# A fourth staging place for split weight halves, from the first output projection on, in a two-layer fp32 backbone on one core

## The chip, the cores and the metric

The kernel runs on one core of a Trainium2 chip. The metric is device time in microseconds (us) of one execution; lower is better. Engines are named as in the profile: PE (TensorE matmul), PEld (its weight loads), DVE (VectorE), ACT (ScalarE), POOL (GpSimd) and SP (SyncE, which issues most DMAs).

## What is computed

Two layers with shared weights are applied to two groups of 128 tokens each (256 columns in all), 2048 channels wide:

```
x = x + g1 * mixer(norm(x) * (1 + sc1) + sh1)      # layer 0: HGRN2 recurrence and gMLP, then w_out
                                                    # layer 1: 2-D DFT ("Fourier"), then w_out
up = h @ w_up                                       # 2048 -> 2*5632
conv = pad[:-2]*cw[0] + pad[1:-1]*cw[1] + pad[2:]*cw[2] + cb
gate, val = split(conv);  x = x + g2 * ((silu(gate) * val) @ w_down)
mod = silu(cond) @ mod_w + mod_b                    # sh, sc, g of each layer: 2048 -> 12288
```

A final RMSNorm ends it. Everything is fp32.

## The kernel before

**Weights as a stream.** All weights pass once from HBM through SBUF. A *unit* is a 128x2048 fp32 tile (1 MB, two *halves* of 128x1024), loaded by SP into one of four `raw` places, five from `open_late` on. For accuracy each half is split in two before the matmuls: ACT copies it rounded to fp32r into `wh` (L169), DVE subtracts to get the rest, `wl` (L170). One half then feeds 24 matmuls of 128x256 (L810, function `t_products`): for each of 4 column blocks and 2 row blocks, `wh` with the high part of the activations, `wh` with the low part, `wl` with the high part. `wh` and `wl` have HL_BUFS = 3 places each, so that the copy into a place waits until PE has finished the half that was there.

**Order of the work.** `Stream.run` (L118) walks over the list of steps and emits instructions. Ahead of a half's matmuls it emits the splits of the halves after it (L200: `while state["split"] < min(len(todo), done + HL_BUFS)`). The framework's scheduler then orders each engine's queue; each engine runs its queue in that order. `loads` (L129) puts the next unit into a `raw` place as soon as all that reads the place has been emitted; SP's queue is in order too.

**Other users of the stream.** The modulation weights are units as well. Some go to PE (L455, "mod units"), 60 of the late ones go to DVE: two *pieces* per unit (L470, a multiply-and-sum over 128x2048), which hold the `raw` place until the second piece is done. One piece is emitted per half, ordered behind the latest split (`next_slow`).

**Stages from the change on** (us from the span's start, read from the trace): first output projection from about 495, FFN of layer 0 from 590 to 1402 (three rounds of up groups and a down projection, the down rounds at about 787 to 910, 1094 to 1186 and 1336 to 1402), Fourier stage 1402 to 1455, second output projection to 1550, FFN of layer 1 to 2330, final norm.

**In an FFN up group** the convolution reads a padded tile `z` (three of them, rotated) into a tile `c` (C_BUFS = 4 of them): one ACT and two DVE instructions (L1384, L1388). ACT's silu, two POOL products (L1450, L1453, tile `gate`) and a split into `G` (L716 on ACT, L717 on DVE) follow. In a projection, ACT scales the sums (L1326) and DVE adds them to X (L1328).

**Scratch in the `late` pool** (opened by `open_late` when the mixers' memory is given back): `cw`, `pos` (the position matrices of the Fourier stage), `z`, `raw4`, four `sq4` tiles (squares for the norm), `uy`/`gate`, four `c`, `junk`, two `a3` and two `odd` (Fourier stage).

Of the kernel before, what the change touches and what calls it, by code (L numbers as in the profile page):

```python
# [18 lines left out]
P = 128  # L19
D = 2048  # L20
KD = D // P
T = 256
# [57 lines left out]
class Stream:  # L80
# [2 lines left out]


    def __init__(self, tc, raw_pool, hl_pool):
        self.tc, self.nc, self.hl_pool = tc, tc.nc, hl_pool
        self.last_split = None
        self.pools = {"early": None, "quarter": None}
        self.bufs = {"early": EARLY_BUFS, "quarter": 1}

        self.slots = deque(dict(pool=raw_pool, tag=f"raw{i}", unit=None) for i in range(RAW_BUFS))
        self.steps = []
        self.units = []
        self.place = self.first = 0
        self.bg = deque()
        self.tails = deque()
        self.soon = deque()
        self.slow = deque()
        self.flags = set()
# [23 lines left out]
    def run(self):  # L123
# [37 lines left out]
        def split_next():  # L161
            s = todo[state["split"]]
            raw = s["u"]["tile"]
            if raw is None:
                return False
            wh = self.hl_pool.tile([P, 2, 512], F32R, tag="wh", name="wh")
            wl = self.hl_pool.tile([P, 2, 512], F32R, tag="wl", name="wl")
            r = raw[:, s["half"] * 1024 : (s["half"] + 1) * 1024].rearrange("p (k n) -> p k n", k=2)
            nc.scalar.copy(out=wh, in_=r)  # L169
            self.last_split = nc.vector.tensor_tensor(out=wl, in0=r, in1=wh.bitcast(F32), op=ALU.subtract).ins  # L170
            s["w"] = (wh, wl)
            state["split"] += 1
            used(s)
            return True
# [8 lines left out]
        for s in self.steps:  # L183
# [5 lines left out]
            elif s["kind"] == "raw":  # L189
                loaded(s)  # L190
                s["fn"](s["u"]["tile"])
                used(s)
            elif s["kind"] == "pieces":
                loaded(s)
                pieces, end = s["fn"](s["u"]["tile"])
                self.slow.extend(pieces[:-1])
                self.slow.append(lambda f=pieces[-1], s=s: (f(), used(s)))
                if end:
                    self.slow.append(end)
            else:  # L200
                while state["split"] < min(len(todo), done + HL_BUFS) and split_next():
                    pass
                while "w" not in s:
                    if not split_next():
                        self.next_slow() if self.slow else self.soon.popleft()()
                if s["pre"]:
                    s["pre"]()
                s["fn"](*s.pop("w"))
                done += 1
                for _ in range(1 + (len(self.soon) > 3)):  # L210
                    if self.soon:
                        self.soon.popleft()()
                if self.slow:
                    self.next_slow()
                self.some()
# [43 lines left out]
def backbone_kernel(ctx: ExitStack, tc: tile.TileContext, a: dict):  # L259
# [1 line left out]

    const = ctx.enter_context(tc.tile_pool(name="const", bufs=1))
    raw_pool = ctx.enter_context(tc.tile_pool(name="raw", bufs=1))
    hl_pool = ctx.enter_context(tc.tile_pool(name="hl", bufs=HL_BUFS))
    tmp = ctx.enter_context(tc.tile_pool(name="tmp", bufs=2))
    acc_pool = ctx.enter_context(tc.tile_pool(name="acc", bufs=ACC_BUFS, space=PSUM))
    misc_pool = ctx.enter_context(tc.tile_pool(name="misc", bufs=MISC_BUFS, space=PSUM))
# [329 lines left out]
    def add_square(t):  # L597
# [1 line left out]
        if t == 0:  # L599
            stat["late"] = []  # L600
        if t >= 12:
            sq = late["pool"].tile([P, T], F32, tag="sq4", name="sq4", bufs=4)
            nc.scalar.activation(out=sq, in_=X[:, t], func=AF.Square)
            stat["late"].append(sq)
            return
# [752 lines left out]
    def open_late():  # L1358

        late["pool"] = ctx.enter_context(tc.tile_pool(name="late", bufs=2))  # L1360
        st.slots.append(dict(pool=late["pool"], tag="raw4", unit=None))
        late["cw"] = late["pool"].tile([P, 2 * 88 * 4], F32, name="cw", bufs=1)
        nc.sync.dma_start(out=late["cw"], in_=a["cw"])
        late["pos"] = late["pool"].tile([P, 3, P], F32, name="pos", bufs=1)
        nc.sync.dma_start(out=late["pos"], in_=a["pos"])
        cond_rows()
        late["zs"] = deque()
        for i in range(3):
            z = late["pool"].tile([P, 2, 260], F32, name=f"z{i}", bufs=1)
            nc.gpsimd.memset(z, 0.0)  # L1370
            late["zs"].append(z)

    def put_ffn(layer):
        cw0 = layer * 88 * 4
# [3 lines left out]

        def conv(z, ft):

            c = late["pool"].tile([P, 260], F32, tag="c", name="c", bufs=C_BUFS)
            w = cw0 + 4 * ft
            o = c[:, 0:258]
            nc.scalar.activation(  # L1384
# [97 lines left out]
    def put_fourier():  # L1482
# [4 lines left out]
        def dft(raw):  # L1487
            d.append(late["pool"].tile([P, 2, 4, 256], F32R, tag="wide", name="dft", bufs=1))
            split_pair(d[0], raw[:, 0:1024].rearrange("p (k n) -> p k n", k=4))

        st.call(st.finish_slow)
        st.unit(a["dft"], [dict(kind="raw", fn=dft)])

        def stage1(n):
# [12 lines left out]
                        skip_group_check=True,  # L1507
                    )
            ab = late["pool"].tile([P, 516], F32, tag="gate", name="ab")
            a3 = late["pool"].tile([P, P], F32, tag="a3", name="a3")  # L1510
            nc.scalar.copy(out=ab[:, 0:128], in_=ps[:, 0:128])
            nc.gpsimd.memset(ab[:, 128:129], 0.0)
            nc.scalar.copy(out=ab[:, 129:512], in_=ps[:, 129:512])
# [4 lines left out]
        def stage2(n, ab, a3):  # L1518
# [16 lines left out]
                        stop=(j == len(parts) - 1),  # L1535
                    )
            s = slice(g * P, (g + 1) * P)
            odd = late["pool"].tile([P, 2, P], F32, tag="odd", name="odd")
            nc.scalar.copy(out=odd[:, 1], in_=y[:, 3 * P : 4 * P])
            nc.vector.tensor_tensor(out=odd[:, 0], in0=y[:, 2 * P : 3 * P], in1=odd[:, 1], op=ALU.add)  # L1540
            nc.vector.tensor_tensor(out=odd[:, 1], in0=y[:, 2 * P : 3 * P], in1=odd[:, 1], op=ALU.subtract)
# [26 lines left out]
        for n in range(9):  # L1568
            st.call(lambda n=n: step(n))
            for _ in range(FNET_MODS[n]):  # L1570
                put_mod("raw")
        st.call(cond_rows)

    def finish():
# [183 lines left out]
```

## Time and profile before

| | |
|---|---|
| three runs | 2347.5, 2352.22, 2356.18 us (median 2352.22) |
| the profiled execution | 2348.72 us, its span 2346.9 us |
| PE busy | 2284.4 us (97%) |
| PE weight loads busy | 2126.6 us (91%) |
| DVE busy | 1684.5 us (72%) |
| ACT busy | 1245.1 us (53%) |
| POOL busy | 393.8 us (17%) |
| DMA | 590 MB, 251 GB/s over the span |

Busy is the time in which an engine has at least one instruction running. Matmuls overlap in PE's pipeline, so its idle time alone does not tell how many matmuls a wait has cost. Between rows of a timeline the start times show the pace.

### The profile page before, as it was taken

How to read it: one execution, taken by the hardware profiler on the slowest of the kernel's cores; microseconds unless marked ns; L12 is line 12 of the kernel's file. 1: busy time of each engine (PE TensorE's matmuls, PEld its weight loads, DVE VectorE, ACT ScalarE, POOL GpSimd, SP SyncE). 2: the span in 40 equal slices, each digit the busy share in tenths (PEclk: the TensorE clock that was granted, in tenths of full speed). 3: DMA queues.
4: the chain of work that ended last, by engine and by line, in shares of the span. 5: the costliest groups of instructions: out<-in, count | busy, mean ns of one | idle time of the engine just before them, and what ended most of it. 6: DMA issues, size and time to landing. Idle time of an engine off the chain costs nothing.

```text
span 2346.9 us, 44307 instructions
## 1 busy us (share of the span) xinstructions
PE 2284.4 (97%) x18316; PEld 2126.6 (91%) x18316; DVE 1684.5 (72%) x2370; ACT 1245.1 (53%) x2052; POOL 393.8 (17%) x427
## 2 busy tenths in 40 slices
PE   6999999999999999999999999999999999999997
PEld 4788878788999999999999986999999999999997
DVE  4558977756878887888888777778884556545664
ACT  5337755554755544555455545566554555545554
POOL 0002321322211101110001151222120011100123
PEclk9999999999999999999999999999999999999998
DMA  8977778788567787777877778755665555555552
GB/s 344 390 299 273 262 288 311 265 347 298 197 236 268 258 310 276 270 268 269 307 283 274 268 260 344 280 204 202 235 246 197 180 181 180 183 187 187 181 180 73
DMA packets 88123, 590.09 MB, mean 251 GB/s; under 512 B 9840, under 2 KB 12272, under 8 KB 20336
## 3 DMA queue, kind: packets, MB, share of 16 engines
q1 hardware_dynamic: 84896, 582.01, 66.6%
q10 hardware_dynamic: 3024, 5.24, 0.6%
q8 instruction: 143, 2.34, 0.4%
q14 instruction: 60, 0.49, 0.1%
HBM read 584.07 MB, written 3.15 MB: 250 GB/s over the span
## 4 chain that ended last, share of the span: by engine, by line
PE 80%; DVE 8%; DMA 3%; POOL 3%; ACT 3%; issue 2%; SPq 0%; DVEq 0%; POOLq 0%; ACTq 0%
PE acc L810 69%; PE acc L841 3%; PE modacc L455 3%; DVE wl L170 3%; DVE junk L470 2%; ACT wh L169 1%; PE modacc L403 1%; POOL gate L1450 1%; DMA raw<-in_down 1%; DVE junk L492 1%; PE acc L826 1%; DMA rows<-in_crow 1%; DMA raw<-in_w_out 1%; DVE c L1388 0%; DVE HS L717 0%
## 5 line engine op out<-in xcount | busy, mean ns | idle before, releaser
L810 PE MATMUL acc<-HS,wh 128*128 128x256 f32 x6656 | 1217.6, 285 | 10.5 <-DVE ush L1402 4.9
L170 DVE TENSOR_TENSOR wl<-raw,wh 128x1024 fp32r<-128x1024 f32 x704 | 872.6, 1246 | 409.3 <-ACT wh L169 406.2
L169 ACT CAST wh<-raw 128x1024 fp32r<-128x1024 f32 x704 | 733.7, 1047 | 711.7 <-PE acc L810 549.0
L810 PEld LDWEIGHTS acc<-HS,wh 128*128 128x128 f32 x6656 | 1031.5, 190 | 55.4 <-issue 37.3
L810 PE MATMUL acc<-HS,wl 128*128 128x256 f32 x3328 | 941.4, 283 | 4.0 <-DVE wl L170 3.9
L810 PE MATMUL acc<-G,wh 128*128 128x256 f32 x3840 | 695.8, 284 | 0.1
L810 PEld LDWEIGHTS acc<-HS,wl 128*128 128x128 f32 x3328 | 635.1, 191 | 7.4 <-DVE wl L170 7.1
L810 PEld LDWEIGHTS acc<-G,wh 128*128 128x128 f32 x3840 | 597.5, 192 | 23.7 <-issue 15.9
L810 PE MATMUL acc<-G,wl 128*128 128x256 f32 x1920 | 544.0, 284 | 7.6 <-DVE wl L170 7.4
L810 PEld LDWEIGHTS acc<-G,wl 128*128 128x128 f32 x1920 | 367.5, 192 | 13.7 <-DVE wl L170 13.7
L1450 POOL TENSOR_TENSOR gate<-gate,c 128x128 f32<-128x128 f32 x88 | 98.2, 1116 | 1232.2 <-DVE c L1388 1160.4
L470 DVE SCALAR_TENSOR_TENSOR junk<-raw,rows 128x2048 bf16<-128x2048 f32 x120 | 276.7, 2306 | 0.0
L1388 DVE SCALAR_TENSOR_TENSOR c<-z,cw,c 128x258 f32<-128x258 f32 x352 | 171.3, 520 | 18.2 <-ACT c L1384 15.8
L716 ACT CAST G<-gate 128x256 fp32r<-128x256 f32 x88 | 35.8, 407 | 140.5 <-POOL gate L1453 138.4
L455 PE MATMUL modacc<-raw,cs 128*32 128x512 f32 x704 | 102.8, 613 | 0.4 <-DMA raw<-in_mod 0.4
L1384 ACT ACTIVATE c<-z,cw 128x258 f32<-128x258 f32 x176 | 102.5, 614 | 0.0
L1326 ACT ACTIVATE acc<-acc,mods 128x128 f32<-128x128 f32 x240 | 81.3, 342 | 36.3 <-PE acc L810 30.9
L841 PE MATMUL acc<-wh,HS 128*128 128x512 f32 x256 | 85.7, 404 | 0.0
L492 DVE SCALAR_TENSOR_TENSOR junk<-quarter,rows 128x512 bf16<-128x512 f32 x96 | 73.8, 768 | 14.2 <-DMA quarter<-in_modq 7.8
L717 DVE TENSOR_TENSOR G<-gate,G 128x256 fp32r<-128x256 f32 x88 | 44.9, 511 | 52.6 <-ACT G L716 52.6
L607 POOL TENSOR_TENSOR sq<-X 128x256 f32<-128x256 f32 x48 | 50.1, 1062 | 186.8 <-DVE X L1328 186.8
L723 POOL TENSOR_TENSOR h<-X,rstd 128x256 f32<-128x256 f32 x44 | 41.2, 945 | 239.3 <-DVE HS L717 208.8
(197 smaller groups left out, 1458.0 us busy)
## 6 DMA issues: line engine op xcount, KB each, us to landing
raw<-in_up SPq DMA_DIRECT2D x176, 1024.0 KB, 4.9
raw<-in_mod SPq DMA_DIRECT2D x150, 1024.0 KB, 5.8
raw<-in_down SPq DMA_DIRECT2D x88, 1024.0 KB, 4.8
raw<-in_w_in SPq DMA_DIRECT2D x49, 1024.0 KB, 6.8
raw<-in_w_out SPq DMA_DIRECT2D x32, 1024.0 KB, 7.0
early<-in_mod SPq DMA_DIRECT2D x30, 1024.0 KB, 10.0
quarter<-in_modq SPq DMA_DIRECT2D x24, 512.0 KB, 3.9
raw<-in_w_in SPq DMA_DIRECT2D x14, 512.0 KB, 10.9
```

The lines of the kernel that those rows point to most:

```text
L169: nc.scalar.copy(out=wh, in_=r)
L170: self.last_split = nc.vector.tensor_tensor(out=wl, in0=r, in1=wh.bitcast(F32), op=ALU.subtract).ins
L455: nc.tensor.matmul(ps[0][32 * j : 32 * j + 32, :], lhsT=cs[:, 4 * u + j, 3 - cg : 35 - cg], rhs=raw[:, 512 * j : 512 * j + 512], start=fir ...
L470: nc.vector.scalar_tensor_tensor(out=junk, in0=raw, scalar=1.0, in1=late["rows"][:, g], op0=ALU.mult, op1=ALU.mult, accum_out=mods[:, s, g ...
L492: nc.vector.scalar_tensor_tensor(out=junk, in0=raw[:, 512 * i : 512 * i + 512], scalar=1.0, in1=mx["rows"][:, g], op0=ALU.mult, op1=ALU.mu ...
L607: nc.gpsimd.tensor_tensor(out=sq, in0=X[:, t], in1=X[:, t], op=ALU.mult)
L810: nc.tensor.matmul(ps[b][:, jj * T : (jj + 1) * T], lhsT=w[:, i, c], rhs=rhs(kt)[:, xs], start=(kt == first and n == 0 and jj == 0), stop= ...
L841: nc.tensor.matmul(ps[g][:, :], lhsT=rhs(kt)[:, xs], rhs=w[:, i, :], start=(kt == first and n == 0), stop=(kt == last and n == 2),)
L1326: nc.scalar.activation(out=ps[b][:, s], in_=ps[b][:, s], func=AF.Identity, scale=by)
L1384: nc.scalar.activation(out=o, in_=z[:, 1:259], func=AF.Identity, scale=tap(w + 1), bias=tap(w + 3))
L1388: nc.vector.scalar_tensor_tensor(out=o, in0=z[:, i : i + 258], scalar=tap(w + i), in1=o, op0=ALU.mult, op1=ALU.add)
L1450: nc.gpsimd.tensor_tensor(out=y[:, 0:P], in0=sg[:, 0:P], in1=cv[j + 2][:, 0:P], op=ALU.mult)
```

## The change

From `open_late` on there is a fourth place for `wh` and `wl`. The places become a rotating list of (pool, number), to which `open_late` adds one in the `late` pool, at the front; the splits ahead of a half are emitted up to the list's length. The 8 KB per partition are found by putting `sq4`, `a3` and `odd` into the four `c` tiles, and `pos` into the `z` tile that stands first in the rotation: it is loaded by a DMA on ACT's queue ahead of the Fourier stage (SP loaded it in `open_late` before), and POOL clears that tile behind the stage.

```diff
+        self.split_in = deque((hl_pool, i) for i in range(HL_BUFS))
...
-            wh = self.hl_pool.tile([P, 2, 512], F32R, tag="wh", name="wh")
-            wl = self.hl_pool.tile([P, 2, 512], F32R, tag="wl", name="wl")
+            pool, i = self.split_in[0]
+            self.split_in.rotate(-1)
+            wh = pool.tile([P, 2, 512], F32R, tag=f"wh{i}", name="wh", bufs=1)
+            wl = pool.tile([P, 2, 512], F32R, tag=f"wl{i}", name="wl", bufs=1)
...
-                while state["split"] < min(len(todo), done + HL_BUFS) and split_next():
+                while state["split"] < min(len(todo), done + len(self.split_in)) and split_next():
...
-            sq = late["pool"].tile([P, T], F32, tag="sq4", name="sq4", bufs=4)
+            sq = small()[:, 0:T]
...
+        st.split_in.appendleft((late["pool"], HL_BUFS))
...
-        late["pos"] = late["pool"].tile([P, 3, P], F32, name="pos", bufs=1)
-        nc.sync.dma_start(out=late["pos"], in_=a["pos"])
...
+    def small():
+        return late["pool"].tile([P, 260], F32, tag="c", name="c", bufs=C_BUFS)
...
+        def positions():
+
+            z = late["zs"][0].rearrange("p k n -> p (k n)")
+            late["pos"] = z[:, 0 : 3 * P].rearrange("p (w n) -> p w n", w=3)
+            nc.scalar.dma_start(out=late["pos"], in_=a["pos"])
+
+        st.call(positions)
...
-            a3 = late["pool"].tile([P, P], F32, tag="a3", name="a3")
+            a3 = small()[:, 0:P]
...
-            odd = late["pool"].tile([P, 2, P], F32, tag="odd", name="odd")
+            odd = small()[:, 0:T].rearrange("p (i n) -> p i n", i=2)
...
+        st.call(lambda: nc.gpsimd.memset(late["zs"][0], 0.0))
```

Lines shift by a few: L169, L170, L470, L716, L1326, L1328 of before are L173, L174, L474, L720, L1330, L1332 of the changed kernel. The numbers in the rows below count buffers as they are made; two splits with the same `raw` number are the halves of one unit.

DVE's queue in the first down round (at about 821 us of the trace of before) holds, before:

```order
L170 TENSOR_TENSOR wl_8791<-raw_8682,wh_8790 128x1024
L170 TENSOR_TENSOR wl_8819<-raw_8682,wh_8818 128x1024
L170 TENSOR_TENSOR wl_8849<-raw_8782,wh_8848 128x1024
L470 SCALAR_TENSOR_TENSOR junk_8876,mods_79<-raw_8648,rows_5000 128x2048
L170 TENSOR_TENSOR wl_8879<-raw_8782,wh_8878 128x1024
L470 SCALAR_TENSOR_TENSOR junk_8908,mods_79<-raw_8648,rows_5000 128x2048
L170 TENSOR_TENSOR wl_8913<-raw_8788,wh_8912 128x1024
L470 SCALAR_TENSOR_TENSOR junk_8940,mods_79<-raw_8754,rows_5000 128x2048
```

and in the changed kernel, where raw_8784 and raw_8790 are the units that were raw_8782 and raw_8788:

```order
L174 TENSOR_TENSOR wl_8793<-raw_8656,wh_8792 128x1024
L174 TENSOR_TENSOR wl_8823<-raw_8784,wh_8822 128x1024
L174 TENSOR_TENSOR wl_8851<-raw_8784,wh_8850 128x1024
L474 SCALAR_TENSOR_TENSOR junk_8880,mods_79<-raw_8650,rows_4998 128x2048
L174 TENSOR_TENSOR wl_8883<-raw_8790,wh_8882 128x1024
L474 SCALAR_TENSOR_TENSOR junk_8910,mods_79<-raw_8650,rows_4998 128x2048
L174 TENSOR_TENSOR wl_8915<-raw_8790,wh_8914 128x1024
L474 SCALAR_TENSOR_TENSOR junk_8944,mods_79<-raw_8719,rows_4998 128x2048
```

The pattern of splits and pieces is the same, but each split is that of the next half: both halves of one unit now stand ahead of the first piece, which stood between them.

ACT's queue at the end of the last up group of that round (at about 799 us) holds, before:

```order
L169 CAST wh_8546<-raw_8395 128x1024
L1449 ACTIVATE gate_8610<-c_8542 128x258
L169 CAST wh_8580<-raw_8435 128x1024
L716 CAST G0_2329<-gate_8610 128x256
L169 CAST wh_8616<-raw_8435 128x1024
L169 CAST wh_8650<-raw_8505 128x1024
```

and in the changed kernel (raw_8437 and raw_8507 were raw_8435 and raw_8505):

```order
L173 CAST wh_8550<-raw_8437 128x1024
L1456 ACTIVATE gate_8614<-c_8546 128x258
L173 CAST wh_8582<-raw_8437 128x1024
L720 CAST G0_2329<-gate_8614 128x256
L173 CAST wh_8620<-raw_8507 128x1024
L173 CAST wh_8652<-raw_8507 128x1024
```

Here too the places in the queue are the same and each copy is that of the next half: ahead of the L716 that waits for POOL, both halves of the unit are copied where one was.

ACT's queue at the start of the second output projection (at about 1454 us) holds, before:

```order
L169 CAST wh_15889<-raw_15807 128x1024
L169 CAST wh_15893<-raw_15807 128x1024
L169 CAST wh_15899<-raw_15850 128x1024
L169 CAST wh_15939<-raw_15850 128x1024
L169 CAST wh_15969<-raw_15878 128x1024
L169 CAST wh_15997<-raw_15878 128x1024
L535 ACT_TABLE_LOAD
```

and in the changed kernel:

```order
L173 CAST wh_15889<-raw_15806 128x1024
L173 CAST wh_15893<-raw_15806 128x1024
L173 CAST wh_15899<-raw_15849 128x1024
L173 CAST wh_15903<-raw_15849 128x1024
L173 CAST wh_15945<-raw_15877 128x1024
L173 CAST wh_15973<-raw_15877 128x1024
L539 ACT_TABLE_LOAD
```

Six copies stand ahead of the table load in both, but the fourth (wh_15903 for wh_15939) now belongs to the group that is emitted ahead of the first matmuls and has a free place.

## Rows read from the trace of the kernel before

**Rows 1.** The page: busy us of each engine, its share of the span, instructions.
```profile
PE 2284.4 (97%) x18316; PEld 2126.6 (91%) x18316; DVE 1684.5 (72%) x2370; ACT 1245.1 (53%) x2052; POOL 393.8 (17%) x427
```
**Rows 2.** Waits of PE from 495 us to the end: tile and line that waited <- what ended the wait: us in total, times, longest.
```profile
PE acc L810 <- DVE wl L170: 8.3, 19, 1.3
PE acc L810 <- DVE ush L1402: 4.9, 2, 3.5
PE acc L1501 <- ACT HS L716: 3.0, 3, 1.2
```
**Rows 3.** Timeline of PE at 1352 us: start, us from the first start to the last end, instruction, count, [idle before <- what ended it].
```profile
1352.32 0.40 PE L810 MATMUL acc<-G,wh 128*128 128x256 f32 x2
1353.22 0.39 PE L810 MATMUL acc<-G,wl 128*128 128x256 f32 x1 [0.50 <-DVE wl L170]
1353.44 0.40 PE L810 MATMUL acc<-G,wh 128*128 128x256 f32 x2
1353.68 0.28 PE L810 MATMUL acc<-G,wl 128*128 128x256 f32 x1
```
**Rows 4.** The first wait of Rows 2 in stretches of 100 us, in this order: from 500, 800, 900, 1100, 1300, 1400 and 1700 us.
```profile
PE acc L810 <- DVE wl L170: 0.3, 1, 0.3
PE acc L810 <- DVE wl L170: 0.9, 4, 0.2
PE acc L810 <- DVE wl L170: 0.6, 3, 0.2
PE acc L810 <- DVE wl L170: 1.3, 2, 0.7
PE acc L810 <- DVE wl L170: 3.0, 4, 1.3
PE acc L810 <- DVE wl L170: 1.8, 3, 0.8
PE acc L810 <- DVE wl L170: 0.6, 2, 0.3
```
**Rows 5.** Waits of ACT from 495 us to the end.
```profile
ACT wh L169 <- PE acc L810: 495.3, 300, 4.9
ACT G L716 <- POOL gate L1453: 138.4, 86, 4.7
ACT wh L169 <- DMA raw<-in_down: 50.5, 17, 5.7
ACT wh L169 <- DMA raw<-in_w_out: 9.8, 3, 4.5
```
**Rows 6.** Timelines of ACT, DVE and PE at the end of the last up group of the first round.
```profile
805.25 0.41 ACT L716 CAST G<-gate 128x256 fp32r<-128x256 f32 x1 [4.62 <-POOL gate L1453]
805.56 3.13 ACT L169 CAST wh<-raw 128x1024 fp32r<-128x1024 f32 x3
806.64 1.23 DVE L170 TENSOR_TENSOR wl<-raw,wh 128x1024 fp32r<-128x1024 f32 x1 [0.53 <-ACT wh L169]
811.27 0.39 PE L810 MATMUL acc<-G,wl 128*128 128x256 f32 x1 [0.21 <-DVE wl L170]
```
**Rows 7.** Timelines of ACT and DVE in the first down round.
```profile
827.77 2.00 ACT L169 CAST wh<-raw 128x1024 fp32r<-128x1024 f32 x2 [5.69 <-DMA raw<-in_down]
828.85 1.22 DVE L170 TENSOR_TENSOR wl<-raw,wh 128x1024 fp32r<-128x1024 f32 x1 [5.36 <-ACT wh L169]
830.00 2.28 DVE L470 SCALAR_TENSOR_TENSOR junk<-raw,rows 128x2048 bf16<-128x2048 f32 x1
832.21 1.22 DVE L170 TENSOR_TENSOR wl<-raw,wh 128x1024 fp32r<-128x1024 f32 x1
```
**Rows 8.** Timeline of DVE in the third down round.
```profile
1348.00 1.23 DVE L170 TENSOR_TENSOR wl<-raw,wh 128x1024 fp32r<-128x1024 f32 x1 [3.37 <-ACT wh L169]
1353.08 2.70 DVE L470 SCALAR_TENSOR_TENSOR junk<-raw,rows 128x2048 bf16<-128x2048 f32 x1
1355.71 1.62 DVE L170 TENSOR_TENSOR wl<-raw,wh 128x1024 fp32r<-128x1024 f32 x1
1357.26 2.81 DVE L470 SCALAR_TENSOR_TENSOR junk<-raw,rows 128x2048 bf16<-128x2048 f32 x1
1360.01 1.75 DVE L170 TENSOR_TENSOR wl<-raw,wh 128x1024 fp32r<-128x1024 f32 x1
```
**Rows 9.** Timelines of ACT and PE at the start of the second output projection.
```profile
1453.90 3.10 ACT L169 CAST wh<-raw 128x1024 fp32r<-128x1024 f32 x3
1456.52 0.39 PE L810 MATMUL acc<-G,wl 128*128 128x256 f32 x1 [0.78 <-DVE wl L170]
1469.90 3.62 ACT L535 ACTIVATE rows<-rows 128x4096 f32<-128x4096 f32 x1 [2.70 <-DMA rows<-in_crow]
```
**Rows 10.** Stretches: busy us of PE, PEld, DVE, ACT and POOL with instruction counts, PEclk, DMA share, GB/s; and from the page's costliest groups the mod units' matmuls (busy, mean ns).
```profile
1750.00:2330.00 580.00, 579.42 (x4816) 579.14 (x4815) 334.37 (x377) 305.94 (x504) 67.23 (x84) 1.00 0.50 177
L455 PE MATMUL modacc<-raw,cs 128*32 128x512 f32 x704 | 102.8, 613 | 0.4 <-DMA raw<-in_mod 0.4
```
**Rows 11.** Timelines of DVE and ACT near the end of the last but one up group of layer 0, and the clearing of the three `z` tiles by POOL (busy, mean ns).
```profile
1309.49 0.47 DVE L1388 SCALAR_TENSOR_TENSOR c<-z,cw,c 128x258 f32<-128x258 f32 x1
1311.05 0.41 ACT L716 CAST G<-gate 128x256 fp32r<-128x256 f32 x1 [2.47 <-POOL gate L1453]
L1370 POOL MEMSET z<- 128x520 f32 x3 | 1.5, 532 | 0.1
```

More of the change, by code (lines that the diff above doesn't have):

```diff
@@ L85, in __init__ @@
     def __init__(self, tc, raw_pool, hl_pool):
-        self.tc, self.nc, self.hl_pool = tc, tc.nc, hl_pool
+        self.tc, self.nc = tc, tc.nc
+        self.split_in = deque((hl_pool, i) for i in range(HL_BUFS))
         self.last_split = None
@@ L263, in backbone_kernel @@
     raw_pool = ctx.enter_context(tc.tile_pool(name="raw", bufs=1))
-    hl_pool = ctx.enter_context(tc.tile_pool(name="hl", bufs=HL_BUFS))
+    hl_pool = ctx.enter_context(tc.tile_pool(name="hl", bufs=1))
     tmp = ctx.enter_context(tc.tile_pool(name="tmp", bufs=2))
@@ L1379, in conv @@
         def conv(z, ft):
-            c = late["pool"].tile([P, 260], F32, tag="c", name="c", bufs=C_BUFS)
+            c = small()
             w = cw0 + 4 * ft
```

## The prediction, made before the changed kernel was run

> **What bounds the kernel now.** The page comes first: PE is busy 97% of the span [rows 1]. Its own waits come next, since only they can give anything back. From 495 us on, where the fourth place exists, PE waits 19 times for `wl`, 8.3 us in all, and the other waits are for work that the change leaves in its order: the evacuation of the first up group (4.9 us) and the Fourier stage's activations (3.0 us) [rows 2]. So the kernel is bound by PE, and what a deeper staging can win lies in those 19 waits.
>
> Idle time is not the whole of a wait. In the timeline two matmuls take 0.24 us from start to start, 0.12 each, though one lasts 0.28; the `wl` matmul at 1353.22 follows `wh` matmuls that began at 1352.32, so it came 0.90 - 0.24 = 0.66 us late, of which 0.50 is shown as idle, and the next start is 0.22 behind it instead of 0.12 [rows 3]. Each wait thus costs its idle time plus 0.16 + 0.10 = 0.26 us. Rows 4 list the waits by stretch; with 0.26 each they cost, from 500 us: 0.56; from 800: 1.94; from 900: 1.38; from 1100: 1.82; from 1300: 4.04; from 1400: 2.58; from 1700: 1.12. That is 13.4 us, the most that the fourth place can take away directly [rows 4].
>
> A half takes PE 24 x 0.12 = 2.88 us [rows 3]. That is also what a further place can add to the lead of the splits. The longest single wait, 1.3 + 0.26 us, is shorter [rows 2], but several follow each other, so what delays the splits has to be looked at stretch by stretch. Behind 1750 us PE starts 4816 matmuls in 580 us, again 0.12 us each, without a gap worth naming [rows 10]: that quarter of the kernel cannot move.
>
> **What the change does to the splits.** ACT copies a half when PE has left its place; 300 of its waits (495.3 us) are that one [rows 5]. With three places the copy for the third half waits for the half before the running one; with four, the copy for the fourth half waits for the same moment. The orders of the queues show it: the pattern stays, the split is that of the next half. So splits come 2.88 us earlier for PE wherever the place was what they waited for. Where the weights themselves are late, nothing comes earlier: 20 waits of ACT, 60.3 us, are for the DMA of projection weights [rows 5]. That gives three kinds of stretches.
>
> *Behind a blocked ACT.* In an up group ACT's queue stands up to 4.7 us at L716, waiting for POOL's product, 86 times [rows 5]; the splits behind it are late. At 805.25 such a wait ends, three copies follow, and PE waits at 811.27 [rows 6]. The raw data are there, so one half more in store covers it. Of the waits from 800 us one is of this kind (0.21 + 0.26 = 0.47 us), and I count those from 900 (1.38) and from 1700 (1.12) to it, as both stand in up groups: 2.97 us, all gained. In the second output projection ACT waits 2.70 us for a DMA and then computes 3.62 us at L535 [rows 9]; the two waits of PE that follow are covered too: 2.58 less the first one, 0.78 + 0.26 = 1.04, leaves 1.54 us. That first one stays: it stands where the splits begin after the Fourier stage, at 1453.90, and PE has nothing to run on before [rows 9].
>
> *Weights late, then DVE full.* In the down rounds two DVE pieces per unit (2.28 us each) hold the raw places. At 827.77 ACT has waited 5.69 us for a DMA; from 828.85 DVE does split, piece, split, piece, 1.15 + 2.21 = 3.36 us for each half where PE takes 2.88 [rows 7]. The DMA comes no earlier after the change, so the first of those waits stays. But two splits now stand ahead of the first piece: the second is ready at about 828.85 + 2 x 1.15 = 831.2 instead of 833.4, PE asks for it at about 830.1 + 2.9 = 833.0, and a lead of 1.8 us carries over the 0.48 us that each of the next halves loses. Of the remaining 1.94 - 0.47 = 1.47 us the first wait (about 0.4) stays: 1.1 gained. The second down round (1.82 us) has the same pattern with longer pieces of other work between, and its first half was in time, so I take all of it. In the third, POOL's squares run beside DVE and pieces take 2.70 and 2.81 us, splits 1.62 and 1.75 [rows 8]. From 1348.00 the new order gives halves at 1349.2, 1350.4, then behind pieces 1353.9, 1358.2 and 1362.8; PE, which began the second at 1352.32 [rows 3], asks every 2.88 us: at 1349.4, 1352.3, 1355.2, 1358.1 and 1361.0. The fifth is 1.8 us late, and the one after about 0.6 more: of 4.04 us some 1.7 are gained.
>
> *The start.* Of the 0.56 us from 500, half: SP has one DMA (`pos`) less ahead of the weights there; 0.3 us.
>
> Sum: 2.97 + 1.54 + 1.1 + 1.8 + 1.7 + 0.3 = 9.4 us.
>
> **What it adds.** No matmul, split or piece is added or taken away. One DMA issue moves from SP to ACT. It waits for the last DVE reading of its `z` tile and stands, in the new order, ahead of the L716 which ACT awaits until 1311.05 anyway; that DVE instruction ends at 1309.96, so it is covered by an idle 2.47 us; without that cover it would cost ACT at most those 2.47 us once, and behind it wait one copy and one L716, inside the lead of a half [rows 11]. POOL clears one tile, 0.53 us, between the Fourier stage and its next squares [rows 11]; POOL is busy 17% [rows 1] and PE does not wait for it there: nothing. The first use of the new place waits for the mixers' last reading of that memory; the steps have emitted all of it before, so I take nothing, at most one half, 2.88 us, once. The shared `c` tiles: in the order in which they are taken, `a3` and `odd` alternate, so each tile comes back after as many steps as with two own ones, and the squares are read before the first convolution. I cost that at nothing; the Fourier queues are reordered slightly, though, and PE's 3.0 us of waits there [rows 2] may become nothing or double: the bounds are -3 and +3 us.
>
> Against the profiled execution's 2348.7 the sum gives 2339.3. The runs' median is 2352.2, 3.5 above that execution; 2352.2 - 9.4 = 2342.8, and I predict 2342.5.
>
> **A rule weighed.** The page gives weight loads 91% against 97% for the matmuls [rows 1]. Perfetto Trace Analysis of the Trainium skill, section Identifying the Most-Contended Engine, says that matmul busy time is no good measure of the headroom on TensorE and that LDWEIGHTS busy time is; by it, PE would have some 220 us to give. Hanging on this: the trace agrees where PE is undisturbed, since loads reach 579.14 of 580 us there [rows 10], but but the 704 mod matmuls (102.8 us busy), which have a quarter of the columns to load, fill nearly half of the difference [rows 10], and the pace of 0.12 us between waits leaves no hidden gap [rows 3]. What the rest would give is a rival below.
>
> **The rivals.**
> *All waits for `wl` go* (0.24): the down rounds recover too, since the extra half is built up before the late DMA. For it: no wait is longer than the 2.88 us gained. Against: ACT waits for raw data just there. 2352.2 - 13.4 = 2338.8.
> *Only the blocked-ACT stretches gain* (0.20): in the down rounds DVE and the raw places decide, not the order. 2.97 + 1.54 = 4.5; 2347.7.
> *Slower* (0.07): in the down rounds a piece now stands behind two splits, 1.15 us later; it holds its raw place as much longer, and if the next unit's DMA is the late one, that is later too. 20 late copies [rows 5] x 1.22 us = 24.4, less 9.4, is 15 us more: 2367. It decides if more than 8 of the 20 pass their delay on to PE. Against: the units whose place is freed by a split, not by a piece, are now loaded earlier.
> *It does nothing* (0.04): the copies that matter wait for data, never for a place; 2352.
> *More than the waits show* (0.02): weight loads are idle for 2346.9 - 2126.6 = 220 us [rows 1]; less the mod matmuls' 102.8 [rows 10] that is 117 us, and if the part behind 495 us, 79%, were all held up by late splits, 93 us could go: 2259. Against it stands the even pace between waits.
> The forecast itself has 0.43.
>
> **Range and chances.** From 2352.2 - 13.4 less some 4 us of spread (the runs lie 4 us to either side of their median): 2335; up to no gain with 3 us of spread: 2355. This leaves out the slower case and the tails. A change of 0.5% is 11.8 us, about what a measurement of this kernel tells from none: the second case lies beyond it, mostly, and a part of the forecast with its spread, 0.30 together; slower than that is 0.06; the rest, 0.64, is no difference that can be told.
>
> **What would show it.** The waits of PE for `wl` from 495 us should fall from 8.3 us in 19 to about 2 to 3 us in five or six, at 830, near 1360 and at the first half of the second output projection; none from 900, 1100 and 1700. ACT's waits for raw data should stay near 60 us, those at L716 near 138. The waits for `ush` should keep their 4.9 us. If those for `wl` vanish and the time does not, the wait has moved to the evacuations or the mod units; if ACT's waits for DMA grow by more than 10 us, the slower case is at work.

## The result, and the profile after

| | before | changed |
|---|---|---|
| median of the runs | 2352.47 us (4 runs, 2347.5 to 2356.18) | 2339.1 us (4 runs, 2337.57 to 2341.01) |
| ratio, 95% interval | | 0.9946 [0.9933, 0.9959] |
| profiled execution, its span | 2348.72, 2346.9 us | 2341.01, 2339.2 us |

The change makes the kernel 13.4 us (0.54%) faster. The profiled execution of the changed kernel is its slowest run.

The page of the changed kernel, answering to [rows 1]:

```profile
PE 2281.2 (98%) x18316; PEld 2128.6 (91%) x18316; DVE 1683.0 (72%) x2370; ACT 1241.7 (53%) x2052; POOL 395.0 (17%) x428
```

PE's waits from 495 us to the end, answering to [rows 2]:

```profile
PE acc L814 <- DVE ush L1409: 4.7, 2, 3.4
PE acc L814 <- DVE wl L174: 3.8, 9, 0.8
PE acc L1515 <- ACT HS L720: 2.9, 2, 2.7
PE acc L814 <- ACT wh L173: 0.8, 2, 0.6
```

The waits for `wl` fell from 8.3 us in 19 to 3.8 in 9; `ush` kept its time; waits for `wh`, of which before has none there, are new. By stretch, answering to [rows 4], in this order: from 800, 1100 (two lines), 1300 and 1400 us (two lines); from 500, 900 and 1700 us there is none left.

```profile
PE acc L814 <- DVE wl L174: 1.3, 2, 0.8
PE acc L814 <- DVE wl L174: 1.0, 3, 0.5
PE acc L814 <- ACT wh L173: 0.6, 1, 0.6
PE acc L814 <- DVE wl L174: 0.8, 3, 0.3
PE acc L814 <- DVE wl L174: 0.7, 1, 0.7
PE acc L814 <- ACT wh L173: 0.2, 1, 0.2
```

ACT's waits from 495 us, answering to [rows 5]:

```profile
ACT wh L173 <- PE acc L814: 409.6, 254, 4.7
ACT G L720 <- POOL gate L1460: 133.5, 84, 4.7
ACT wh L173 <- DMA raw<-in_down: 84.4, 20, 8.3
ACT wh L173 <- DMA raw<-in_up: 31.5, 14, 5.1
ACT wh L173 <- DMA raw<-in_w_out: 7.1, 3, 3.3
```

ACT waits 86 us less for a place and 57 us more for raw data: 123.0 us now, 65.8 before (60.3 of them in [rows 5], 5.5 for `in_up`). What held the loads is seen at SP, which issues them in order and stands still until the `raw` place of the next one is free. First two rows of the kernel before, then two of the changed one, 495 to 1750 us:

```profile
SPq L153 <- DVE wl L170: 836.6, 182, 8.7
SPq L153 <- DVE junk L470: 110.7, 59, 4.6
```

```profile
SPq L155 <- DVE wl L174: 546.9, 178, 10.8
SPq L155 <- DVE junk L474: 309.9, 58, 10.1
```

The loads now wait for a place that a piece (`junk`) left last for 309.9 us instead of 110.7, for one that a split left last for 289.7 us less, and for one that PE's mod matmuls left last for 75.0 us more. Whether PE pays for it, these sums do not tell; the experiments have to say.

**Where the time went.** Idle time alone does not give that. I took one instruction that is the same in all kernels, ACT's first scaling (L1326 / L1330) of each projection, and compared its start with the start in before. For instance, timelines of ACT at the first and third down round of layer 1, before and changed:

```profile
1773.53 0.72 ACT L1326 ACTIVATE acc<-acc,mods 128x128 f32<-128x128 f32 x2 [0.51 <-PE acc L810]
2276.05 0.72 ACT L1326 ACTIVATE acc<-acc,mods 128x128 f32<-128x128 f32 x2 [0.51 <-PE acc L810]
```

```profile
1766.64 0.34 ACT L1330 ACTIVATE acc<-acc,mods 128x128 f32<-128x128 f32 x1 [0.50 <-PE acc L814]
2268.64 0.34 ACT L1330 ACTIVATE acc<-acc,mods 128x128 f32<-128x128 f32 x1 [0.51 <-PE acc L814]
```

The changed kernel is 6.89 us ahead at the first and 7.41 at the second. The table gives these differences (us, minus is ahead of before; the last column is the last scaling of all), for the profiled executions of all kernels that keep five or six `raw` places and at least three split places:

| start in before | 504.6 | 809.4 | 1104.7 | 1342.4 | 1480.6 | 1773.5 | 2276.1 | 2329.0 |
|---|---|---|---|---|---|---|---|---|
| changed | 4.2 | 3.2 | 0.3 | -0.3 | -4.9 | -6.9 | -7.4 | -7.7 |
| changed, again | -0.1 | -1.1 | -4.2 | -6.1 | -12.0 | -12.8 | -13.3 | -13.6 |
| sharing alone | 4.2 | 3.6 | 3.7 | 3.7 | 3.3 | 3.2 | 3.2 | 3.2 |
| place in layer 0 only | 4.5 | 3.5 | 1.0 | -0.1 | -4.4 | -3.7 | -3.7 | -3.7 |
| place in layer 1 only | 5.8 | 5.3 | 5.2 | 5.2 | 5.8 | 4.0 | 2.9 | 2.6 |
| sixth raw place | 2.0 | 1.5 | -2.9 | -5.5 | -10.7 | -11.9 | -11.9 | -11.9 |
| before, short pieces | -0.3 | -0.5 | -5.8 | -8.4 | -16.2 | -16.5 | -16.5 | -16.5 |
| changed, short pieces | 3.4 | 2.4 | -3.1 | -5.0 | -12.0 | -14.1 | -14.6 | -14.9 |

The first column stands about where the place is opened, and lies between -0.3 and 5.8 us in kernels that differ little up to there. By so much single executions can differ at the start: the changed kernel has 4.2 us there in one execution and -0.1 in the other. The granted clock goes with it. From 20 to 40 us it was 1.00 in before and in the three kernels of the table that stand between -0.3 and 2.0 us ("changed, again" is one), and 0.83 to 0.91 in the five that stand between 3.4 and 5.8. So the changed kernel's profile shows 7.7 us where the medians show 13.4. From 504.6 us on it gains 11.9 us, in the execution "again" 13.5.

### The profile page after: what moved, and what is told of

The parts are those of the page before. It is cut to its first block, busy times and chain, and to the rows that moved or that the text cites. A ratio compares the mean times of both kernels' runs of the same rounds, so it can differ in the third digit from the quotient of the medians.

```text
span 2339.2 us, 44277 instructions
## 1 busy us (share of the span) xinstructions
PE 2281.2 (98%) x18316; PEld 2128.6 (91%) x18316; DVE 1683.0 (72%) x2370; ACT 1241.7 (53%) x2052; POOL 395.0 (17%) x428
## 4 chain that ended last, share of the span: by engine, by line
PE 84%; DVE 7%; DMA 3%; ACT 2%; issue 2%; POOL 2%; SPq 0%; DVEq 0%; ACTq 0%; POOLq 0%
PE acc L814 72%; PE acc L845 4%; PE modacc L459 3%; DVE wl L174 2%; DMA raw<-in_down 2%; DVE junk L474 2%; PE modacc L407 1%; ACT wh L173 1%; DMA raw<-in_w_in 1%; PE acc L830 1%; PE acc L1515 1%; DVE junk L496 1%; DMA early<-in_mod 0%; DVE HS L721 0%; PE misc L1131 0%
## 5 line engine op out<-in xcount | busy, mean ns | idle before, releaser
L814 PE MATMUL acc<-HS,wh 128*128 128x256 f32 x6656 | 1220.2, 285 | 10.2 <-DVE ush L1409 4.7
L174 DVE TENSOR_TENSOR wl<-raw,wh 128x1024 fp32r<-128x1024 f32 x704 | 872.8, 1250 | 398.7 <-ACT wh L173 396.6
L173 ACT CAST wh<-raw 128x1024 fp32r<-128x1024 f32 x704 | 730.6, 1048 | 685.5 <-PE acc L814 462.7
L814 PEld LDWEIGHTS acc<-HS,wh 128*128 128x128 f32 x6656 | 1034.9, 190 | 54.7 <-issue 36.3
L814 PE MATMUL acc<-HS,wl 128*128 128x256 f32 x3328 | 943.2, 284 | 3.3 <-DVE wl L174 3.2
L814 PE MATMUL acc<-G,wh 128*128 128x256 f32 x3840 | 692.7, 283 | 0.8 <-ACT wh L173 0.8
L814 PEld LDWEIGHTS acc<-HS,wl 128*128 128x128 f32 x3328 | 635.7, 191 | 5.8 <-DVE wl L174 5.6
L814 PEld LDWEIGHTS acc<-G,wh 128*128 128x128 f32 x3840 | 594.1, 191 | 24.6 <-issue 15.9
L814 PE MATMUL acc<-G,wl 128*128 128x256 f32 x1920 | 541.7, 283 | 3.8 <-DVE wl L174 3.8
L814 PEld LDWEIGHTS acc<-G,wl 128*128 128x128 f32 x1920 | 365.8, 191 | 6.0 <-DVE wl L174 6.0
L474 DVE SCALAR_TENSOR_TENSOR junk<-raw,rows 128x2048 bf16<-128x2048 f32 x120 | 276.9, 2307 | 0.0
L1330 ACT ACTIVATE acc<-acc,mods 128x128 f32<-128x128 f32 x240 | 80.4, 342 | 56.1 <-PE acc L814 51.2
L720 ACT CAST G<-gate 128x256 fp32r<-128x256 f32 x88 | 35.8, 407 | 135.6 <-POOL gate L1460 133.5
```

The costliest lines, as they stand in the source:

```text
L474: nc.vector.scalar_tensor_tensor(out=junk, in0=raw, scalar=1.0, in1=late["rows"][:, g], op0=ALU.mult, op1=ALU.mult, accum_out=mods[:, s, g ...
L814: nc.tensor.matmul(ps[b][:, jj * T : (jj + 1) * T], lhsT=w[:, i, c], rhs=rhs(kt)[:, xs], start=(kt == first and n == 0 and jj == 0), stop= ...
L1330: nc.scalar.activation(out=ps[b][:, s], in_=ps[b][:, s], func=AF.Identity, scale=by)
```

## Experiments

**The change again, the sharing alone, and the place in one layer.** The four ran on one chip. The second kernel leaves out the line that adds the place:

```diff
-        st.split_in.appendleft((late["pool"], HL_BUFS))
```

the third takes the place out again at the Fourier stage, the fourth adds it behind that stage:

```diff
+        st.call(lambda: st.split_in.remove((late["pool"], HL_BUFS)))
```

```diff
-        st.split_in.appendleft((late["pool"], HL_BUFS))
...
+        st.call(lambda: st.split_in.appendleft((late["pool"], HL_BUFS)))
```

> The changed kernel unaltered, so that the three kernels beside it are compared on one chip. From the two traces (same PE work, start against start): 3.4 us lost ahead of the change's first effect, then gained 2.0 in the first down round, 1.5 in the up groups behind it, 0.4 in the second down round, 3.4 in the third, 1.6 in the second output projection, 2.3 in the FFN of layer 1: 11.2 us. If the 3.4 us at the start are spread, this is 11 us faster than before (2341); if they belong to the change, 8 us (2344).

> Only the scratch sharing, pos on ACT and POOL's clearing; three places for the splits as before. Theory (the place alone gives the time): within 2 us of before, PE waits for wl about 8 us in 19 times from 495 us. Rival (the gain comes with the sharing: one DMA less on SP at the start, other queues in the Fourier stage): 5 us or more faster. Second rival (the sharing costs and hides part of the gain): 2 to 4 us slower.

> The fourth place is taken out of the rotation at the Fourier stage, so the second output projection and the FFN of layer 1 have three. Theory (each stretch gains by itself): 2.0 + 1.5 + 0.4 + 3.4 = 7.3 us faster than before, the wl waits of the second output projection and at 1700 us back. Rival (down rounds gain nothing, only blocked-ACT stretches): 1.5 us. Rival (a lead won early is kept to the end): as fast as the changed kernel.

> The fourth place comes into the rotation only behind the Fourier stage. Theory (each stretch gains by itself): 1.6 + 2.3 = 3.9 us faster than before, wl waits of the down rounds of layer 0 as before. Rival (what layer 0 gains is spread): nearly as fast as the changed kernel.

Measured, before on the same chip 2353.14 us: again 2339.4 us, ratio 0.994 [0.9928, 0.9953]; sharing alone 2351.85, 0.9996 [0.9987, 1.0004]; layer 0 only 2343.93, 0.9954 [0.9941, 0.9967]; layer 1 only 2347.41, 0.9975 [0.9966, 0.9984]. PE's waits for `wl` with the sharing alone:

```profile
PE acc L814 <- DVE wl L174: 7.5, 17, 1.3
```

The changed kernel again has 4.0 us of waits for `wl` in 9, and none for `wh`. The place alone makes the gain; sharing, `pos` on ACT and POOL's clearing cost and win nothing that can be told. The two halves, 9.2 and 5.7 us, add up to the whole within the intervals, and the table shows each gain in the layer that has the place. The waits for `wl` of the down rounds of layer 0 are back in the fourth kernel, the two at 1700 us in the third. The two at the table load in the second projection are away in both: in the third ACT stood there 1.35 us for `in_crow` instead of 2.70 [rows 9], in the fourth 4.16 us, with the place.

**The same 8 KB as a sixth raw place, and the raw place given up for a fifth split place.**

```diff
-        st.split_in.appendleft((late["pool"], HL_BUFS))
...
+        st.slots.append(dict(pool=late["pool"], tag="raw5", unit=None))
```

```diff
-        st.slots.append(dict(pool=late["pool"], tag="raw4", unit=None))
+        st.split_in.appendleft((late["pool"], HL_BUFS + 1))
```

> The same 8 KB as a sixth place for raw units; three places for the splits. Theory (two causes: in the up groups and the second output projection the splits stand behind a blocked ACT and need their own depth; in the down rounds raw data are late): the waits of the blocked stretches stay (900, 1400, 1700 us: about 5 us with their refill), those of the down rounds go in part: 2 to 6 us faster than before, ACT's waits for in_down well below the 50 us of before. Rival (only the depth of the splits counts, everywhere): within 1.5 us of before. Rival (bytes staged count, in whatever form): as fast as the changed kernel, 13 us.

> The fifth raw place is given to a fifth place for splits. Theory (with four places for splits the down rounds are bound by loads that start late, since the raw places are all taken by units that wait for pieces): the down rounds lose, 3 us or more slower than the changed kernel, more waits of PE for wl and wh in the down rounds than its 8, none in the blocked stretches. Rival (depth of the splits is what counts): as fast as the changed kernel or up to 4 us faster, as its remaining waits go.

Measured: 2337.2 us, 0.9934 [0.9921, 0.9946], and 2465.89 us, 1.0487 [1.0472, 1.0501]. With the sixth raw place, PE's waits for `wl` and SP's waits for pieces:

```profile
PE acc L814 <- DVE wl L174: 3.6, 7, 1.3
SPq L155 <- DVE junk L474: 121.2, 60, 9.0
```

My theory gave the sixth raw place 2 to 6 us; it won 15.7, no less than the fourth split place can be told to win. It takes away waits that I had put down to a blocked ACT: from 900 us one of 0.2 us stays of 3 (as does the one at 811), and the two of the second output projection behind its first half are gone, where ACT no longer stands for `in_crow` at all. Those at 1700 us stay (0.5 us in 2). ACT's waits for `in_down` have vanished, while those at L720 are what they were at L716 (136.5 us, longest 4.7). The other trade shows that bytes staged are not the rule either, as all three kernels stage 72 KB per partition (8 KB in each place): with four raw and five split places the loss is 126 us against the changed kernel, by more than the "3 us or more" of the theory and out of reach of the rival. In that kernel PE waits for both kinds of split from 495 us on:

```profile
PE acc L814 <- ACT wh L173: 59.8, 26, 6.3
PE acc L814 <- DVE wl L174: 19.3, 35, 2.4
```

and the granted clock falls where a wait is some us long. Between 920 and 1000 us the longest, 3.4 us, ends at 936.8 us; stretches of it, columns as in [rows 10]:

```profile
920.00:930.00 10.00, 10.00 (x84) 9.03 (x83) 6.18 (x5) 2.00 (x2) 0.00 (x0) 1.00 0.32 111
930.00:940.00 10.00, 6.06 (x42) 5.65 (x41) 5.58 (x7) 5.50 (x11) 0.00 (x0) 0.91 0.67 282
940.00:950.00 10.00, 9.26 (x67) 8.76 (x67) 6.24 (x6) 3.04 (x3) 0.00 (x0) 0.92 0.60 210
```

The waits are 79.1 us. The mean granted clock over the span of 2464.2 us is 0.976 against 0.992 in the changed kernel, so part of the loss is time at the lower of the two levels, 1.2 GHz, behind such waits. As an estimate from these rows, the clock costs (0.992 - 0.976) x 2464.2 = 39 us and the 61 waits, at 0.26 us each beside their idle time, 79.1 + 15.9 = 95 us, where the 11 of the changed kernel cost 7.5: together that is the loss, about.

**Short pieces.** Each of the 120 pieces reads 256 of its 2048 columns, before and with the change; the modulation sums leave out the rest:

```diff
-                    out=junk,
-                    in0=raw,
+                    out=junk[:, 0:256],
+                    in0=raw[:, 0:256],
...
-                    in1=late["rows"][:, g],
+                    in1=late["rows"][:, g, 0:256],
```

> The kernel before, with each of the 120 pieces on DVE cut to 256 of 2048 columns, some 0.3 us instead of 2.3; the modulation sums leave out the rest of the columns. Theory (in the down rounds the pieces fill DVE and hold raw places): the wl waits of the down rounds go, those of the blocked stretches stay: 5 to 8 us faster than before. Rival (pieces have no part in it): same as before.

> The changed kernel with the same short pieces; the same sums are left out. Theory: the fourth place is then worth only what it covers behind a blocked ACT, 3 to 5 us between the two kernels with short pieces, and PE's wl waits are below 1.5 us. Rival (the place is worth the same whatever DVE does): 11 us or more between the two.

Measured: 2334.47 us, 0.992 [0.9907, 0.9934], and 2333.8 us, 0.9922 [0.9909, 0.9936]. A piece took 0.45 us instead of 2.3. PE's waits for `wl` and ACT's for POOL, before with short pieces, then changed with short pieces:

```profile
PE acc L810 <- DVE wl L170: 1.1, 2, 0.8
ACT G L716 <- POOL gate L1453: 97.7, 82, 2.4
```

```profile
PE acc L814 <- DVE wl L174: 0.8, 1, 0.8
ACT G L720 <- POOL gate L1460: 97.6, 82, 2.4
```

Both theories miss: before gains 18.4 us rather than 5 to 8, and the place is then worth nothing (0.7 us between the medians, well inside the intervals), rather than 3 to 5 us. With short pieces 17 of the 19 waits are gone without the fourth place, those at 900 and 1700 us and in the second output projection among them. So the waits behind a blocked ACT have to do with the pieces too: ACT's wait for POOL itself falls, from 138.4 us with a longest of 4.7 [rows 5] to 97.7 and 2.4. SP's waits for pieces are longer with short ones (297.6 us before, 424.9 with the change), while ACT's for raw data fall to 19.5 and 48.3 us: what left a place last does not tell whether the data came in time. A new order of the queues came with the shorter pieces, PE's included (see the goes of the mod units below), so not every us of the 18.4 is the pieces' own time.

**Fewer raw places, fewer split places.** Four raw places with four and with three split places (the lines for `raw4` and for the place taken out); six raw places with two split places (one taken out of the list); and four raw with five split places and short pieces.

> The changed kernel without its fifth raw place: four places for raw units, four for splits. Theory (the number of raw places decides, since units that wait for pieces hold them, and a split place makes up for a raw place only while raw data are at hand): within 15 us of the kernel with four raw and five split places (2466). Rival (it was the fifth split place that did the harm there): 2340 to 2380.

> Four places for raw units, three for splits. Theory (the number of raw places decides): within 15 us of the two kernels with four raw places and more split places. Rival (bytes staged decide, in whatever form): 13 us slower again than with four split places.

> Six raw places, two for splits: the other end of the trade. Theory (raw places cover late data only; a split behind a piece takes 1.15 + 2.21 = 3.36 us where PE has 2.88 for a half, and with two places nothing is in store): 0.5 us or more lost at most of the 120 pieces, 60 us or more slower than before. Rival (the splits' depth matters little once the raw data are there): within 10 us of before.

> Four raw and five split places, with the pieces on DVE cut to 256 of 2048 columns; the modulation sums leave out the rest. Theory (the pieces hold the raw places): most of the loss of the same places with full pieces (126 us over the changed kernel) goes, 2370 or less. Rival (four raw places are too few for the loads' 5 to 9 us anyway): 2420 or more.

Measured, with all the others that have full pieces (median us, ratio to before):

| raw places | 2 split | 3 split | 4 split | 5 split |
|---|---|---|---|---|
| 4 | | 2391.8 (1.0172) | 2430.0 (1.0323) | 2465.9 (1.0487) |
| 5 | | 2352.5 | 2339.1 (0.9946) | |
| 6 | 2441.7 (1.0383) | 2337.2 (0.9934) | | |

With short pieces, four raw and five split places take 2398.31 us (1.0191 [1.017, 1.0212]).

With four raw places each further split place costs 36 to 38 us. Neither theory nor rival had that: I had expected the three kernels within 15 us of one another, the rivals 2340 to 2380 us with four split places and a gain with the bytes. ACT's waits for raw data and PE's for `wh`, with four raw places and three, then four split places:

```profile
ACT wh L173 <- DMA raw<-in_down: 71.4, 16, 10.7
ACT wh L173 <- DMA raw<-in_up: 59.5, 24, 6.8
PE acc L814 <- ACT wh L173: 21.8, 11, 4.7
SPq L155 <- DVE junk L474: 106.0, 56, 4.6
```

```profile
ACT wh L173 <- DMA raw<-in_down: 102.2, 23, 9.9
ACT wh L173 <- DMA raw<-in_up: 80.4, 33, 7.6
PE acc L814 <- ACT wh L173: 34.8, 23, 2.7
SPq L155 <- DVE junk L474: 322.4, 54, 12.4
```

From three to four split places SP's waits (495 to 1750 us again) for pieces rise by 216 us, as they do with five raw places (by 199), but here the raw data come too late for PE. The loss is of the kind that the slower rival had: ACT's waits for raw data pass on to PE. My reading, which no run shows by itself, is that splits that run further ahead need raw data sooner, while the units for pieces and for the mod matmuls stay in their places for as long as before. With five split places SP's waits for pieces are short again (84.1 us) and the kernel is slower still, so SP's sum by itself does not rank the kernels. Short pieces take back 68 of the 126 us, a little over half: the result, 2398, lies between theory and rival. The other half is not the pieces' length; that it is the mod units of PE, which stay in place too, was not tried. With two split places the time is as the theory had it, 90 us slower than the 2351.33 of its own chip, but its reason, a split behind a piece, is not all of it: of PE's 92 waits for `wl`, 32 (12.4 us) come after 1818.6 us, when the last of the 120 pieces has ended.

```profile
PE acc L814 <- DVE wl L174: 53.8, 92, 2.1
```

## Why the prediction was right, and where it was not

**The time** (2342.5, range 2335 to 2355) held: 2339.1 and 2339.4. The likeliest outcome by the 0.5% bound was "no difference" and the median fell just beyond it, as the sum was 4 us short. As predicted, a longer lead of the splits took waits for `wl` away; what was wrong are the sizes of terms, the cause of some, and one term put at nothing.

**What the change adds** was rightly put at nothing: 0.9996 [0.9987, 1.0004] for the sharing alone.

**The sum by stretch**, against the table (changed, and changed again): the start 0.3, measured 1.0 and 1.0, of which the sharing alone has 0.5. First down round and the up groups behind it 0.47 + 1.1 + 1.38 = 2.95, measured 2.9 and 3.1. Second round 1.8, measured 0.6 and 1.9. Third round up to the start of the second projection 1.7 + 1.54 = 3.24, measured 4.6 and 5.8. From there to the first down round of layer 1 1.12, measured 2.0 and 0.8. Behind that nothing, measured 0.8 and 0.8. Nine waits for `wl` stayed, not five or six.

**A term put at nothing: the order of PE's own work.** "No matmul, split or piece is added or taken away" is so, but the order of PE's queue changed too. In each of the three down rounds of layer 0 the kernel before has the eight matmuls of one mod unit in two goes, at two spots of the queue, the changed kernel in one, and a go of two lasts as long as one of eight. Two rows of before, then one of the changed kernel:

```profile
843.48 1.05 PE L455 MATMUL modacc<-raw,cs 128*32 128x512 f32 x2
849.91 1.06 PE L455 MATMUL modacc<-raw,cs 128*32 128x512 f32 x6
```

```profile
851.51 1.07 PE L459 MATMUL modacc<-raw,cs 128*32 128x512 f32 x8
```

For the same 80 and 64 of these matmuls PE is busy 11.70 us from 809 to 1105 us and 9.57 from 1105 to 1343 before, and 10.66 and 8.53 with the change; with the third round's that is 3.1 us. The sharing alone and the place in layer 1 only have the two goes of before; the place in layer 0 only, the sixth raw place and both kernels with short pieces have one. So 3.1 us of their gains is no wait for `wl` at all, and it is luck that the 2.95 us of the first down round and the up groups behind it came out: the waits there give 1.5 and 1.7 us by the price of 0.26, the go 1.04. No run changed this order by itself.

**The third round was undersized.** Of the 4.6 and 5.8 us, 1.04 is a go of mod matmuls. The order of the splits came as predicted, two splits ahead of the pieces. DVE's timeline of the changed kernel, answering to [rows 8]:

```profile
1347.04 2.94 DVE L174 TENSOR_TENSOR wl<-raw,wh 128x1024 fp32r<-128x1024 f32 x2 [1.26 <-ACT wh L173]
1349.90 2.82 DVE L474 SCALAR_TENSOR_TENSOR junk<-raw,rows 128x2048 bf16<-128x2048 f32 x1
1352.66 1.75 DVE L174 TENSOR_TENSOR wl<-raw,wh 128x1024 fp32r<-128x1024 f32 x1
1354.33 2.28 DVE L474 SCALAR_TENSOR_TENSOR junk<-raw,rows 128x2048 bf16<-128x2048 f32 x1
1356.54 1.21 DVE L174 TENSOR_TENSOR wl<-raw,wh 128x1024 fp32r<-128x1024 f32 x1
1357.68 2.28 DVE L474 SCALAR_TENSOR_TENSOR junk<-raw,rows 128x2048 bf16<-128x2048 f32 x1
1359.89 1.22 DVE L174 TENSOR_TENSOR wl<-raw,wh 128x1024 fp32r<-128x1024 f32 x1
```

The second to fifth half are ready at 1349.98, 1354.41, 1357.75 and 1361.11, where I had 1350.4, 1353.9, 1358.2 and 1362.8. The step that failed is the duration of the pieces: I took them from before with POOL's squares beside them (2.70 and 2.81 us). One piece still takes 2.82 and the split behind it 1.75, the next pieces 2.28 and the splits behind them 1.2: the squares and sums of POOL beside which they were slow, from 1352.11 to 1360.67 us before, now run from 1346.72 to 1353.32, since DVE's addition to X that they wait for stands ahead of the pieces. From the second half to the fifth that is 11.1 us where I had 12.4, and the second came 0.4 earlier: 1.7 us at the fifth, for which PE waits 0.2 us, not 1.8. The longest wait of the round is 0.3 us, in the execution "again" 1.0, further on. The two executions differ in the Fourier stage: PE goes 53.17 us without a matmul of L810 there before, 53.96 (L814) with the change and 52.25 again, and from 1400 to 1420 us the granted clock was 1.00, 0.74 and 0.91. With the change PE was busy for 1.36 of the 4 us from 1408, and in the next 4 us the clock stood at the lower level, 0.50.

**The second round was oversized, since raw data were late.** I took all 1.82 us of its waits, as its first half had been in time; with the change 1.6 us of waits stay there, and again 0.6, so that by the price of 0.26 its waits cost 0.8 us more and 0.4 less than before, and the go of mod matmuls, 1.04 us, is the larger part of the 0.6 and 1.9. "The DMA comes no earlier" was said of the first round and is too kind to the second: the data come later relative to what ACT asks for. ACT and PE of the changed kernel at 1166 us:

```profile
1165.70 2.00 ACT L173 CAST wh<-raw 128x1024 fp32r<-128x1024 f32 x2 [8.31 <-DMA raw<-in_down]
1166.80 0.74 PE L814 MATMUL acc<-G,wh 128*128 128x256 f32 x4 [0.60 <-ACT wh L173]
1168.06 0.39 PE L814 MATMUL acc<-G,wl 128*128 128x256 f32 x1 [0.52 <-DVE wl L174]
```

ACT has stood 8.31 us for a unit of `in_down`; what was in store did not last as long, and PE waits for `wh`. "ACT's waits for raw data should stay near 60 us" was wrong (123.0, again 98.5), and a growth by more than 10 us, named as the sign of the slower case, came with a faster kernel: an off-path wait is a sign only where PE's own rows follow it. With five raw places they do for 0.8 us (not at all in the execution "again"), with four for tens. The slower rival's 24.4 us used 1.22 us for a delay of 1.15, which makes 23.0.

**Blocked ACT was given too much as a cause** (4.5 us of the 9.4). The place takes all eight of these waits away, as predicted. But with three split places and raw data in time, the sixth raw place, ACT stands at L720 as long as before, and only four of the eight are left: one at 812 us, one at 933 and two at 1700, 0.9 us and with 0.26 each 1.9. These are the blocked ones. The other four, two from 900 us and two in the second projection, needed earlier loads, or the place. Even the blocked ones have to do with the pieces: with short ones ACT's longest wait for POOL is 2.4 us, and none of the eight is left.

**The most that the waits can give** (13.4 us) did not bound what staging can gain: the kernel before with short pieces gains 16.2 us from 504.6 us on. By the price of 0.26 us beside the idle time, the 11 waits that stay cost 3.8 + 0.8 + 2.9 = 7.5 us; of 13.2 for the 19 of [rows 2] that leaves 5.7, where 11.9 were gained; again, 9 waits of 4.0 us leave 6.9 of 13.5. The sixth raw place gained 13.8 from 504.6 us on with 7 waits for `wl` left. Of the surplus 3.1 us are the goes of the mod units and up to 1.9 a faster pace (last section); that leaves 1.2 and 1.6 us for which I have no row. So the sum came out near the truth with terms that were too small and one premise too many; the rival "all waits for `wl` go" (2338.8) gave nearly the measured time, but not the rows.

**More than the waits show** did not come about in the form given. With short pieces PE has 0.8 us of waits for `wl` left in the changed kernel, and the weight loads' idle time is its span, 2332.0, less

```profile
PE 2278.5 (98%) x18316; PEld 2127.5 (91%) x18316; DVE 1486.9 (64%) x2370; ACT 1244.8 (53%) x2052; POOL 360.8 (15%) x428
```

that is 204.5 us, where before had 220.3; what these runs changed in the staging reached 16 of them. The Trainium skill (Perfetto Trace Analysis, section Identifying the Most-Contended Engine) judges TensorE's headroom by MFU (the share of its peak arithmetic rate that a kernel uses) and by the busy share of LDWEIGHTS, the weight loads; by the second, an estimate, some 200 us would still be left to win here, which no run here shows.

## What to carry to other kernels

Size staging from both ends and for the whole stream: a deeper second stage helps only while the first can deliver, and what stands in the first stage for another engine (here units for DVE's pieces) counts as taken. Compare also what the bounding engine itself does, go by go: a change of the queues can save it work that no list of waits shows. When a wait is put down to a cause, shorten the suspected cause itself before believing it: one run with short pieces told more than all the timelines. A longer wait on an engine off the path is no loss by itself; look for the row of the bounding engine that follows it.

## What the runs showed of the hardware that was not expected

The stretch from the first to the third down round of layer 1 takes 2276.05 - 1773.53 = 502.52 us before and 2268.64 - 1766.64 = 502.00 us with the change, though PE waits for no semaphore there in either. It is 502.52 or 502.51 in the four other kernels of the table without a fourth split place there, and 501.5 to 502.0 in those with it. If all 1825 us from 504.6 us on run faster by that 0.1%, it is 1.9 us of the gain. What makes the matmuls' pace depend on the place was not found.

Of the mod units' matmuls, two in a go keep PE as long as eight (1.05 and 1.07 us in the rows above), so breaking a unit into two goes cost 1.04 us each time.
